# Block 0's down-projection added by ScalarE copies and DMA additions, and the attention's bias made later in seven pieces

## The chip, the cores and the metric

The kernel runs on one core of one Trainium2 chip. The metric is the device time of one execution in microseconds (us), given as a median of several runs. Lower is better. The engines are named as the profile names them: PE is TensorE, DVE is VectorE, ACT is ScalarE, POOL is GpSimd, and SP is the queue that issues most loads.

## The reference

A decoder trunk of two layers on one sequence of 512 tokens with 1024 features, all in float32. Each layer does, in this order:

```python
x = x + 0.5 * swiglu(rms_norm(x, ffn1_norm[l]), ffn1_wg[l], ffn1_wu[l], ffn1_wd[l])
h = rms_norm(x, mix_norm[l]); z = h @ w_in[l]      # [q | k | v | conv_B | conv_C | conv_h]
x = x + concat([attention(q, k, v, sink), short_conv(B, C, h_conv)]) @ w_out[l]
x = x + 0.5 * swiglu(rms_norm(x, ffn2_norm[l]), ffn2_wg[l], ffn2_wu[l], ffn2_wd[l])
```

and a final `rms_norm` ends it. `swiglu(h, wg, wu, wd)` is `(silu(h @ wg) * (h @ wu)) @ wd` with 2816 inner features. The attention has 8 query heads, works in blocks of 128 tokens with a window of 128, and adds to the scores a bias that depends on the head and on the distance of query and key alone; keys outside the window get a very large negative number. That bias, 8 heads x 128 queries x 256 keys, is made once by the kernel.

## The kernel before

The stream x lies in SBUF with features on partitions: eight tiles `xs[c]` of 128 features x 512 tokens. Every product is done with float32 split in two parts (high and low, `hi` and `lo`), three matmuls for one: weights are split by `split` (L224: an ACT cast makes `wh`, a DVE subtraction makes `wl`), activations likewise.

**The stages of a SwiGLU.** `INNER` lists them: `p` (two blocks of 128 inner features done plainly), `d (0,)` (block 0's part of the down-projection, eight column results of 128 features, three matmuls per row chunk), then five stages `w` 1, 3, 5, 7, 9, two `s` stages and a last `d`. A stage `w` is a product of gate and up weights done with seven products in place of eight (`winograd2`, in the order of `CHAINS`: operands b11, b21, t2, t3, t1, t4, b22). Each of its seven products has two halves of 12 matmuls (L806), 168 in all. This text calls the stages w1, w3, w5. The first products of a `w` stage are added up in PSUM under the names `x` (tag `mm`), `w` (tag `aux`) and `y` (tag `sc`); tags `sc` and `aux` have two buffers each.

**Block 0's down-projection in the first SwiGLU.** `down(rhs, fresh=True)` yields eight results `acc`. The first four lie in tag `mm`, the last four in `sc`, `sc`, `aux`, `aux`. For each, DVE does `xs[c] = 0.5 * acc + xs[c]` (L1228), and between them the operands of w1 are made (`norm.make`: half-size sums on DVE at L587 to L592, splits at L224). The normed input is scaled on DVE at L536 just before. The stream is next read or written in the last stages of the same SwiGLU: what the `s` stages yield is kept apart (`Apart`) and added at the end.

**The weights.** Each `w` stage needs ten weight tiles of 512 KB; `need_raw` loads them by SP (L207) some tiles ahead, and sums of two weight blocks are made by a second DMA issued by POOL which adds to the tile in SBUF (L219), or by DVE (L263, L283). There are eight tiles (`raw`), three `wh` and three `wl`. `take_split` hands out the next split and has the splits of two groups ahead traced. `state["rest"]` is the last DVE subtraction of a split that was traced; `tc.issue_after(i)` queues what the block traces for an engine behind instruction `i` on that engine. For all else a scheduler decides at build time, from the order in which instructions are traced and from its own estimates, in what order each engine gets them; each engine then works through its list in order.

**The attention's bias.** `make_bias` (L769 to L782) makes it: an iota on POOL (L771), a conversion on DVE (L773), two masks and their sum (L776 to L778), and eight operations, one for each head (L780). It is traced at once ahead of w3 in the first SwiGLU (`late()`, where `b == 3`). Its first reader is the attention of the first layer, after that SwiGLU.

Temporary tiles come from `g2` (14 buffers of 128 x 512 float32) and `nsq` (2 buffers of that size, used by the squares of the norms).

Of the kernel before, what the change touches and what calls it, by code (L numbers as in the profile page):

```python
# [8 lines left out]
F32 = mybir.dt.float32  # L9
# [3 lines left out]
I32 = mybir.dt.int32  # L13
AF = mybir.ActivationFunctionType
ALU = mybir.AluOpType

P = 128
# [4 lines left out]
NH = 8  # L22
# [5 lines left out]
FAR = -3.0e38  # L28
# [4 lines left out]
INNER = (  # L33
    ("p", 0), ("d", (0,)), ("w", 1), ("w", 3), ("w", 5), ("w", 7), ("w", 9), ("s", 1), ("s", 5),
    ("d", (9, 10)),
)
# [37 lines left out]
def trunk_kernel(  # L74
# [23 lines left out]
    nc = tc.nc  # L98
# [5 lines left out]
    work = ctx.enter_context(tc.tile_pool(name="work", bufs=1))  # L104
# [5 lines left out]
    def g2(name, dt=F32, shape=(P, S)):  # L110
        return work.tile(list(shape), dt, tag="g2", bufs=14, name=name)
# [63 lines left out]
    def turn_rows(i):  # L175
        n = rows[i].shape[0]
        rp = psum("aux", [P, n], f"par_ps{i}")
        nc.tensor.transpose(rp, rows[i], ident[:n, :n])
        nc.scalar.copy(par[:, 16 * i : 16 * i + n], rp)
# [15 lines left out]
    state = {"raw": 0, "split": 0, "group": 0, "late": None}  # L195
# [228 lines left out]
    xs = [xpair[c // 2][:, c % 2, :] for c in range(KC)]  # L424
# [181 lines left out]
    norm = Norm(0)  # L606
# [159 lines left out]
    bias_f = const.tile([P, NH * P], F32, name="bias")  # L766
    bias = bias_f.bitcast(BF16).rearrange("p (h k) -> p h k", h=NH)

    def make_bias():  # L769
        di = g2("dist_i", I32, (P, 2 * P))  # L770
        nc.gpsimd.iota(di, pattern=[[-1, 2 * P]], base=P, channel_multiplier=1)  # L771
        df = g2("dist", F32, (P, 2 * P))
        nc.vector.tensor_copy(df, di)  # L773
        m0 = g2("mask0", F32, (P, 2 * P))
        m1 = g2("mask1", F32, (P, 2 * P))
        nc.vector.tensor_scalar(m0, df, 0.0, FAR, op0=ALU.is_lt, op1=ALU.mult)  # L776
        nc.vector.tensor_scalar(m1, df, float(P), FAR, op0=ALU.is_ge, op1=ALU.mult)
        nc.vector.tensor_add(m0, m0, m1)  # L778
        for h in range(NH):
            nc.vector.scalar_tensor_tensor(  # L780
                bias[:, h, :], df, -(2.0 ** -(h + 1)), m0, op0=ALU.mult, op1=ALU.add
            )  # L782

    def stand(accs, wh, wl, xh, xl, h, start):

# [124 lines left out]
    def ahead(ops, at):  # L910
        return lambda step: ops.make(*at.get(step, ()))


    def ffn(norm, stages, after=None, late=None):
# [207 lines left out]
        def shared(b):  # L1122
            return Seven(lambda: [raws[b], raws[b + 2]], room_form, f"s_{norm.i}_{b}")

        def joined(between):


            def step(n):
                if n == 3:
                    crossing[0].join_half(0)  # L1130
                if n == 4:
                    crossing.pop(0).join_half(1)
                if crossing and isinstance(crossing[-1], Tail):
                    crossing[-1].during(n)
                between(n)

            return step
# [17 lines left out]
        def flush(n=1, *tag):  # L1155
            for _ in range(n):
                if pending:
                    pending.pop(0)(*tag)

        end = None  # L1160
        kept = {}
        apart = Apart(f"{norm.i}")
        for i, (what, b) in enumerate(stages):
            if what == "w" and stages[i + 1][0] == "s":
                ops = shared(sevens[0])
                winograd2(b, ahead(ops, {3: ("b11",), 4: ("b21",), 5: ("t2",), 6: ("t3",)}))
            elif what == "w":
                if late and b == 3:
                    late()
                if after is None and b == 1:  # L1170
                    end = apart = Finale()
                winograd2(b, end and b == 1 and end.step)
            if what == "s" and end:
                ends = [
                    Seven(full, None, f"e_{n}")
                    for n, full in enumerate((lambda b=b: [raws[b + 4], raws[b + 6]], raws[b + 8]))
                ]

                def between(step):
                    if 0 < step < 3:  # L1180
                        flush(2, "mm")
                    for at, n, operand in ((3, 0, "b11"), (4, 1, "b11"), (5, 0, "t2"), (6, 1, "t2")):
                        if step == at:
                            ends[n].make(operand)

                share(ops, 0.5, joined(between), apart, still=kept)
            elif what == "e":
                end.last(ends, kept)
                return
            elif what == "s" and b == sevens[0]:  # L1190
                then = shared(sevens[1])
                share(
                    ops,
                    0.5,
                    joined(ahead(then, {3: ("b11",), 4: ("b21",), 5: ("t2",), 6: ("t3",)})),
                    apart,
                    still=kept,
                )
            elif what == "s":

                def between(step):
                    if step == 1:
                        crossing[0].rejoin(1)
                    if step in (4, 5):
                        with tc.issue_after(state["rest"]):
                            crossing[0].parts(step - 4)
                    if step in SENT_AT:
                        apart.send(*SENT_AT[step])
                    if step == 6:
                        apart.back(1, 1)  # L1210

                share(then, 0.5, between, apart, behind=(0, 2, 3), on=kept)
            if what == "p":
                plain(b)
                if late:
                    turn_rows(1)
            if what != "d":
                continue
            rhs = [(acts[k][0][:, j, :], acts[k][1][:, j, :]) for k in b if k in acts for j in range(2)]
            final = i + 1 == len(stages)  # L1220
            if final:
                after.norm.order = halves_of(KC, 1, True)
            for c, acc in down(rhs, b == (0,), final):
                if b == (0,):
                    made = {0: "b21", 2: "t2", 5: "t3"}
                    if c in made:
                        norm.make(made[c])
                nc.vector.scalar_tensor_tensor(  # L1228
                    xs[c], acc, 0.5, xs[c], op0=ALU.mult, op1=ALU.add
                )  # L1230
                flush()
                if final:
                    for quarter in BACK_AT.get(c, ()):
                        apart.back(*quarter)
                    for k in FINAL_AT.get(c, (c,)):
                        after(k)

    class Finale:
# [7 lines left out]
        def step(self, step):  # L1246


            if step > 2:
                return  # L1250
            for t, tag in (((0, "sc"),), ((1, "sc"),), ((2, "mm"), (3, "aux")))[step]:
                tps = []
                for half in range(2):
                    tp = psum(tag, [P, S], f"yt_{t}_{half}")
                    for j in range(NT):
                        nc.tensor.transpose(
                            tp[:, j * P : (j + 1) * P],
                            xs[half * NT + j][:, t * P : (t + 1) * P],
                            ident,
                        )  # L1260
                    tps.append(tp)
                if t == 0:
                    self.y.append([bias_f[:, half * S : (half + 1) * S] for half in range(2)])
                if t == 1:
                    self.y.append([g2(f"ytok{t}_{half}") for half in range(2)])
                if t > 1:
                    self.late.append(tps)
                else:
                    for half in range(2):
                        nc.scalar.copy(self.y[t][half], tps[half])  # L1270
            if step == 2:
                for t, tps in zip((2, 3), self.late):
                    room = xpool.tile([P, 2, S], F32, tag=f"x{t}", name=f"ytok{t}")
                    self.y.append([room[:, half, :] for half in range(2)])
                    for half in range(2):
                        nc.scalar.copy(self.y[t][half], tps[half])
# [379 lines left out]

    for l in range(DEPTH):
        n1, n2, n3 = Norm(3 * l + 1), Norm(3 * l + 2), Norm(3 * l + 3)
        ffn(norm, INNER, into(n1), None if l else make_bias)
        mix(l, n1, into(n2))  # L1660
        if l + 1 < DEPTH:
            ffn(n2, INNER, into(n3))
        else:
            ffn(n2, LAST)
        norm = n3
# [30 lines left out]
```

## Time and profile before

| | |
|---|---|
| median of 3 runs | 1644.7 us (1643.36 to 1645.09) |
| the profiled execution | 1644.6 us |
| its span, first to last instruction | 1642.8 us |
| granted clock of TensorE | 0.999 |
| DVE busy | 1375.2 us |
| ACT busy | 1169.0 us |
| HBM read | 264.29 MB |

The profile is one execution taken by the hardware profiler. A row of the timeline has start, length, engine, line, operation, output <- inputs, and in brackets how long the engine stood idle before it and who ended that. A row of the waits has who waited on whom, the time in all, how often, and the longest. A row of a line's or a tile's instructions has min/median/max of their length in ns. A row of windows has the stretch, its length, and the busy time of PE, the weight loads, DVE, ACT and POOL in it (instructions in brackets), the clock, the busy share of the DMA engines, and GB/s.

### The profile page before, as it was taken

Reading aid. Unit: us, or ns where it says so; the run is one execution under the profiler, and the core shown is the slowest. Engines: PE = TensorE matmul, PEld = TensorE weight load, DVE = VectorE, ACT = ScalarE, POOL = GpSimd, SP = SyncE. Lnnn points to the kernel's source line nnn. Section 1 sums busy time; section 2 is a strip of 40 time slices with the busy share of each in tenths; the row PEclk is TensorE's granted clock in tenths of the full one; section 3 lists DMA queues with packets and bytes.
Section 4 is the critical chain, followed back from the end, with each engine's and each line's share of the span. In section 5 each row is a group of like instructions: output and inputs, shape, how many; then the busy total and the mean of one; then the engine's idle time right before and its main releaser. Section 6 shows DMA issues by size and latency. Waiting matters only on the chain.

```text
span 1642.8 us, 21157 instructions
## 1 busy us (share of the span) xinstructions
PE 1623.4 (99%) x7588; PEld 1349.7 (82%) x7588; DVE 1375.2 (84%) x1787; ACT 1169.0 (71%) x1498; POOL 216.5 (13%) x191
## 2 busy tenths in 40 slices
PE   9899999999999999999999999999999999999998
PEld 6678888888898888888888888888888988888886
DVE  7977797887899977798999777979788998777997
ACT  6557778766767577777865777788586766777665
POOL 1011111100131011111011111110012111111121
PEclk9999999999999999999999999999999999999999
DMA  9489989932497699999966989998136967999992
GB/s 270 124 209 224 229 212 232 222 100 62 110 222 191 176 227 216 213 214 234 238 150 173 228 208 216 217 230 231 52 90 151 230 146 187 222 222 225 231 266 71
DMA packets 301789, 314.96 MB, mean 192 GB/s; under 512 B 121260, under 2 KB 184308, under 8 KB 301684
## 3 DMA queue, kind: packets, MB, share of 16 engines
q1 hardware_dynamic: 260916, 229.58, 49.6%
q0 software_dynamic: 40048, 83.37, 29.8%
q8 instruction: 59, 0.97, 0.2%
q10 hardware_dynamic: 720, 0.66, 0.1%
q14 instruction: 46, 0.38, 0.1%
HBM read 264.29 MB, written 2.10 MB: 162 GB/s over the span
## 4 chain that ended last, share of the span: by engine, by line
PE 80%; DVE 9%; ACT 5%; DMA 3%; issue 2%; POOL 0%; SPq 0%; ACTq 0%; DVEq 0%; POOLq 0%
PE x L806 25%; PE y L806 13%; PE x_s L806 7%; PE w L806 6%; PE acc L311 4%; PE acc L310 4%; PE acc L313 4%; PE y_s L806 4%; DVE wl L224 3%; PE w_s L806 2%; PE x_m L791 2%; ACT wh L224 1%; PE y_m L791 1%; PE acc L684 1%; PE x_e L806 1%
## 5 line engine op out<-in xcount | busy, mean ns | idle before, releaser
L224 DVE TENSOR_TENSOR wl<-raw,wh 128x1024 fp32r<-128x1024 f32 (+1 forms) x493 | 599.3, 1223 | 176.1 <-ACT wh L224 175.0
L224 ACT CAST wh<-raw 128x1024 fp32r<-128x1024 f32 (+1 forms) x493 | 513.2, 1045 | 307.3 <-PE x L806 100.4
L311 PE MATMUL acc<-xl,wh 128*128 128x512 f32 x392 | 153.4, 391 | 0.3 <-DVE xl L457 0.3
L310 PE MATMUL acc<-xh,wh 128*128 128x512 f32 x392 | 153.1, 392 | 0.5 <-ACT wh L224 0.5
L313 PE MATMUL acc<-xh,wl 128*128 128x512 f32 x384 | 149.8, 390 | 0.0
L219 POOL DMA_DIRECT2D raw<-in_ffn_wu_dram x40 | 50.5, 1270 | 402.7 <-DMA raw<-in_ffn_wu_dram 273.0
L311 PEld LDWEIGHTS acc<-xl,wh 128*128 128x128 f32 x392 | 73.7, 188 | 15.5 <-DVE xl L457 1.0
L310 PEld LDWEIGHTS acc<-xh,wh 128*128 128x128 f32 x392 | 73.8, 188 | 15.2 <-ACT wh L224 0.6
L313 PEld LDWEIGHTS acc<-xh,wl 128*128 128x128 f32 x384 | 72.2, 188 | 14.9
L219 POOL DMA_DIRECT2D raw<-in_ffn_wg_dram x40 | 49.4, 1265 | 201.6 <-DMA raw<-in_ffn_wu_dram 74.9
L219 POOL DMA_DIRECT2D raw<-in_ffn_wd_dram x34 | 41.2, 1220 | 246.3 <-DVE wl L224 103.0
L263 DVE TENSOR_TENSOR raw<-raw,raw 128x1024 f32<-128x1024 f32 x58 | 70.4, 1219 | 3.1 <-DMA raw<-in_ffn_wu_dram 2.6
L806 PE MATMUL w<-wh,fb21h 128*128 128x512 f32 x160 | 62.5, 391 | 2.1 <-DVE x L1228 2.1
L806 PE MATMUL w<-wl,fb21h 128*128 128x512 f32 x160 | 62.3, 391 | 1.5 <-DVE wl L224 1.5
L1068 ACT COPY raw_a<-turned 128x1024 uint16<-128x1024 uint16 x48 | 63.5, 1356 | 0.0
L806 PE MATMUL y<-wh,ft3h 128*128 128x512 f32 x160 | 62.4, 390 | 0.9 <-ACT wh L224 0.9
L806 PE MATMUL x<-wl,ft2h 128*128 128x512 f32 x160 | 62.2, 390 | 1.1 <-DVE wl L224 1.1
L806 PE MATMUL x<-wl,fb11h 128*128 128x512 f32 x160 | 62.2, 390 | 1.0 <-DVE wl L224 1.0
L806 PE MATMUL y<-wh,ft4h 128*128 128x512 f32 x160 | 62.3, 390 | 0.5 <-ACT wh L224 0.5
L806 PE MATMUL x<-wh,ft2h 128*128 128x512 f32 x160 | 62.4, 390 | 0.0
L806 PE MATMUL x<-wh,ft2l 128*128 128x512 f32 x160 | 62.3, 389 | 0.0
L806 PE MATMUL w<-wh,fb21l 128*128 128x512 f32 x160 | 62.3, 389 | 0.0
(501 smaller groups left out, 4532.3 us busy)
## 6 DMA issues: line engine op xcount, KB each, us to landing
raw<-in_ffn_wu_dram SPq DMA_DIRECT2D x127, 512.0 KB, 5.3
raw<-in_ffn_wd_dram SPq DMA_DIRECT2D x105, 512.0 KB, 6.2
raw<-in_ffn_wg_dram SPq DMA_DIRECT2D x86, 512.0 KB, 5.3
raw<-in_ffn_wu_dram POOLq DMA_DIRECT2D x40, 512.0 KB, 8.6
raw<-in_ffn_wg_dram POOLq DMA_DIRECT2D x40, 512.0 KB, 6.1
raw<-in_w_in_dram SPq DMA_DIRECT2D x36, 512.0 KB, 3.8
raw<-in_ffn_wd_dram POOLq DMA_DIRECT2D x34, 512.0 KB, 9.6
raw<-raw POOLq DMA_DIRECT2D x21, 512.0 KB, 7.0
```

What stands on the lines that cost most here:

```text
L219: nc.gpsimd.dma_start(out=r, in_=rows_of(*more), accum_op=ALU.add)
L224: return nc.scalar.copy(hi, raw), eng.tensor_sub(lo, raw, f32(hi))
L263: nc.vector.tensor_add(a11, a11, s1)
L310: nc.tensor.matmul(acc, hi[:, k, :], rhs[k][0], start=k == first, stop=False)
L311: nc.tensor.matmul(acc, hi[:, k, :], rhs[k][1], start=False, stop=False)
L313: nc.tensor.matmul(acc, lo[:, k, :], rhs[k][0], start=False, stop=k == last)
L684: nc.tensor.matmul(opening[n], (lo if part == "w" else hi)[:, k, :], xl if part == "x" else xh, start=n not in begun, stop=k == KC - 1 and ...
L791: nc.tensor.matmul(accs[c // 2][:, c % 2, :], w[:, k, cols], x_[:, 2 * h + k, :], start=start and c % 2 == 0 and h + k + i == 0, stop=h + ...
L806: nc.tensor.matmul(accs[u], x_[:, 2 * h + k, tok], w[:, k, :], start=start and h + k + i == 0, stop=h + k == 2 and i == 2, skip_group_chec ...
L1068: nc.scalar.copy(words(raws[self.b][:, c, :]), self.to[:, :, c, :])
```

## The change

Two things are changed, both in the first SwiGLU of the first layer only.

1. For block 0's down-projection, ACT copies 0.5 * `acc` from PSUM into a new `g2` tile, and a DMA issued by POOL adds that tile to `xs[c]` in SBUF. The DVE instruction stays for all other places.
2. `make_bias` becomes `bias_steps`, which returns a function that `winograd2` calls after each of the seven steps of w5 (`b == 5`). After step 0 it traces the iota, the conversion and the masks; after steps 1 to 6 the heads (0, 1), (2, 3), 4, 5, 6, 7. Each piece's DVE instructions are queued behind the last DVE split traced. `dist` and `mask0` move from `g2` to `nsq`.

```diff
-    def make_bias():
+    def bias_steps():
...
-                if late and b == 3:
-                    late()
                 if after is None and b == 1:
                     end = apart = Finale()
-                winograd2(b, end and b == 1 and end.step)
+                between = late if b == 5 else end.step if end and b == 1 else None
+                winograd2(b, between)
...
-                nc.vector.scalar_tensor_tensor(
-                    xs[c], acc, 0.5, xs[c], op0=ALU.mult, op1=ALU.add
-                )
+                if b == (0,) and norm.i == 0:
+                    part = g2(f"down_{c}")
+                    nc.scalar.activation(part, acc, AF.Copy, scale=0.5)
+                    nc.gpsimd.dma_start(out=xs[c], in_=part, accum_op=ALU.add)
+                else:
+                    nc.vector.scalar_tensor_tensor(
+                        xs[c], acc, 0.5, xs[c], op0=ALU.mult, op1=ALU.add
+                    )
```

The new function, where `masks` holds what `make_bias` did up to the sum of the masks and `heads` the operation of L780:

```python
        def step(n):
            with tc.issue_after(state["rest"]):
                if n == 0:
                    masks()
                else:
                    heads(*((0, 1), (2, 3), (4,), (5,), (6,), (7,))[n - 1])
```

More of the change, by code (lines that the diff above doesn't have):

```diff
@@ L767, in trunk_kernel, with masks, heads, step @@
     bias = bias_f.bitcast(BF16).rearrange("p (h k) -> p h k", h=NH)
-    def make_bias():
[L770 to L781, printed above, removed]
-            )
+    def bias_steps():
+        made = {}
+        def masks():
+            di = g2("dist_i", I32, (P, 2 * P))
+            nc.gpsimd.iota(di, pattern=[[-1, 2 * P]], base=P, channel_multiplier=1)
+            df = work.tile([P, 2 * P], F32, tag="nsq", bufs=2, name="dist")
+            nc.vector.tensor_copy(df, di)
+            m0 = work.tile([P, 2 * P], F32, tag="nsq", bufs=2, name="mask0")
+            m1 = g2("mask1", F32, (P, 2 * P))
+            nc.vector.tensor_scalar(m0, df, 0.0, FAR, op0=ALU.is_lt, op1=ALU.mult)
+            nc.vector.tensor_scalar(m1, df, float(P), FAR, op0=ALU.is_ge, op1=ALU.mult)
+            nc.vector.tensor_add(m0, m0, m1)
+            made["m"] = df, m0
+        def heads(*hs):
+            df, m0 = made["m"]
+            for h in hs:
+                nc.vector.scalar_tensor_tensor(
+                    bias[:, h, :], df, -(2.0 ** -(h + 1)), m0, op0=ALU.mult, op1=ALU.add
+                )
+        def step(n):
+            with tc.issue_after(state["rest"]):
+                if n == 0:
+                    masks()
+                else:
+                    heads(*((0, 1), (2, 3), (4,), (5,), (6,), (7,))[n - 1])
+        return step
     def stand(accs, wh, wl, xh, xl, h, start):
@@ L1227, in ffn @@
                         norm.make(made[c])
-                nc.vector.scalar_tensor_tensor(
-                    xs[c], acc, 0.5, xs[c], op0=ALU.mult, op1=ALU.add
-                )
+                if b == (0,) and norm.i == 0:
+                    part = g2(f"down_{c}")
+                    nc.scalar.activation(part, acc, AF.Copy, scale=0.5)
+                    nc.gpsimd.dma_start(out=xs[c], in_=part, accum_op=ALU.add)
+                else:
+                    nc.vector.scalar_tensor_tensor(
+                        xs[c], acc, 0.5, xs[c], op0=ALU.mult, op1=ALU.add
+                    )
                 flush()
@@ L1658, in trunk_kernel @@
         n1, n2, n3 = Norm(3 * l + 1), Norm(3 * l + 2), Norm(3 * l + 3)
-        ffn(norm, INNER, into(n1), None if l else make_bias)
+        ffn(norm, INNER, into(n1), None if l else bias_steps())
         mix(l, n1, into(n2))
```

## The prediction

> **What bounds the kernel now.** First the page's head, for the size of the field; then busy time by stage of block 0 and the blocks behind it.
>
> ```profile
> span 1642.8 us, 21157 instructions
> PE 1623.4 (99%) x7588; PEld 1349.7 (82%) x7588; DVE 1375.2 (84%) x1787; ACT 1169.0 (71%) x1498; POOL 216.5 (13%) x191
> ```
> ```profile
> 45.40:90.00 44.60, 39.66 (x170) 30.98 (x169) 41.89 (x44) 24.20 (x29) 2.39 (x2) 1.00 0.51 138
> 90.00:130.90 40.90, 38.73 (x170) 31.38 (x169) 31.14 (x41) 27.22 (x32) 5.64 (x6) 1.00 0.87 218
> 130.90:169.00 38.10, 38.10 (x170) 31.56 (x169) 27.71 (x29) 28.12 (x33) 4.90 (x5) 1.00 0.93 221
> ```
>
> TensorE (PE) is busy 99% of the span, so only its gaps can be won: 1642.8 - 1623.4 = 19.4 us in all. The windows are the first three seven-product stages of the first SwiGLU, w1, w3 and w5 (columns after the stretch: its length, busy us of PE, weight loads, VectorE = DVE, ScalarE = ACT, POOL, then clock, DMA share, GB/s). All three do the same 168 matmuls. w5 has no gap; w1 and w3 have 4.9 and 2.2 us. In w1 DVE works 41.89 of 44.60 us, in w5 27.71 of 38.10. A gap costs more than it shows, since the matmuls behind it start slowly; so I take the stages' lengths from PE's timeline, whose first matmul of each of four stages is:
>
> ```profile
> 45.37 0.39 PE L806 MATMUL x<-wh,fb11h 128*128 128x512 f32 x1
> ...
> 89.98 0.39 PE L806 MATMUL x<-wh,fb11h 128*128 128x512 f32 x1
> ...
> 130.88 0.39 PE L806 MATMUL x<-wh,fb11h 128*128 128x512 f32 x1
> ...
> 168.96 0.39 PE L806 MATMUL x<-wh,fb11h 128*128 128x512 f32 x1
> ```
>
> w1 lasts 44.61, w3 40.90, w5 38.08 us. Against w5, w1 loses **6.53** and w3 **2.82**, together 9.35 us: the most that the change can win here. The waits of PE in these stages name who ends them:
>
> ```profile
> PE x L806 <- DVE wl L224: 2.1, 2, 1.1
> PE w L806 <- DVE x L1228: 2.1, 1, 2.1
> PE w L806 <- DVE wl L224: 1.5, 2, 1.1
> PE y L806 <- ACT wh L224: 1.4, 2, 0.9
> ```
>
> The 2.1 on L1228 is the PSUM room of the `w` chain: the last two column results of block 0 sit in it until DVE has added them to the stream. DVE's timeline shows why that is late:
>
> ```profile
> 43.12 1.27 DVE L1228 SCALAR_TENSOR_TENSOR x<-acc,x 128x512 f32<-128x512 f32 x2
> ...
> 46.60 0.68 DVE L1228 SCALAR_TENSOR_TENSOR x<-acc,x 128x512 f32<-128x512 f32 x1
> ...
> 48.93 1.21 DVE L224 TENSOR_TENSOR wl<-raw,wh 128x1024 fp32r<-128x1024 f32 x1
> ...
> 53.00 1.88 DVE L1228 SCALAR_TENSOR_TENSOR x<-acc,x 128x512 f32<-128x512 f32 x3
> ...
> 77.94 1.22 DVE L224 TENSOR_TENSOR wl<-raw,wh 128x1024 fp32r<-128x1024 f32 x1 [1.43 <-ACT wh L224]
> ```
> ```profile
> L1228 DVE SCALAR_TENSOR_TENSOR x<-acc,x 128x512 f32<-128x512 f32 x8 | 5.2, 679 | 0.0
> ```
>
> The second block is the group of these instructions between 40 and 90 us (busy, mean ns, idle before). DVE has not one idle gap in the timeline's stretch before the 1.43 us at 77.94. So w1 is bound by DVE's queue: whatever leaves it brings forward everything behind it.
>
> **The additions.** Removed: the eight L1228 instructions. One lasts 0.68 us, three in a row 1.88 (at 53.00), so they start 0.60 us apart, and 8 x 0.60 = 4.8 us leave DVE. Added: eight ACT copies out of PSUM, and eight DMA additions issued by POOL.
>
> ```profile
> L870 ACT ACTIVATE apart<-x_s x18: 583/596/604, 249.4 to 1091.2; 128x512 f32<-128x512 f32 x18
> ```
> ```profile
> 40.41 1.04 ACT L224 CAST wh<-raw 128x1024 fp32r<-128x1024 f32 x1
> 43.23 1.06 ACT L224 CAST fb21h<-hf 128x1024 fp32r<-128x1024 f32 x1 [1.78 <-DVE hf L536]
> 45.38 1.06 ACT L224 CAST wh<-raw 128x1024 fp32r<-128x1024 f32 x1 [1.10 <-PE acc L311]
> 48.10 1.05 ACT L224 CAST wh<-raw 128x1024 fp32r<-128x1024 f32 x1 [1.66 <-PE x L806]
> ...
> 58.31 1.05 ACT L224 CAST ft1h<-hf 128x1024 fp32r<-128x1024 f32 x1 [5.36 <-DVE hf L590]
> ```
>
> L870 is the same operation on the same shape: 0.596 us, 8 x 0.596 = 4.8 us. ACT is idle 1.78 + 1.10 + 1.66 = 4.5 us between 41.45 and 48.10 and 5.36 us ahead of 58.31, so the copies lie beside other work. They empty PSUM as the columns end (the last just before w1's first matmul at 45.37), so the `w` chain finds its room free. Without that cover a copy ahead of a cast costs 0.6 us.
>
> Is all of the 4.8 us won? The two additions at 43.12 stood where DVE had to wait anyway: the next step needs the cast `fb21h` of 43.23, which ends at 44.29. Their 1.2 us are won only if other ready work moves in. There is some: the `wl` of 48.93 needs the `wh` cast at 40.41, long done, and takes 1.14 us. I take it that it moves in, and subtract 0.1 for an ACT copy ahead of the cast at 45.38: **4.7 us**. The ends: 2.4 (gap not filled, two copies ahead of `fb21h`: 4.8 - 1.2 - 1.2) and 6.53 (the last stalls vanish as well, because DVE falls behind PE less).
>
> POOL and the DMA queues. The rows are POOL's timeline, the nearest DMA addition between SBUF tiles, the software queue of the page, and three 10 us windows:
>
> ```profile
> 39.18 2.47 POOL L219 DMA_DIRECT2D raw<-in_ffn_wg_dram  x2 [2.26 <-DMA raw<-in_ffn_wu_dram]
> 79.52 1.19 POOL L219 DMA_DIRECT2D raw<-in_ffn_wu_dram  x1 [37.88 <-DVE wl L224]
> ```
> ```profile
> L230 POOL DMA_DIRECT2D wl<-raw x10: 856/896/899, 36.0 to 1334.4; - x10
> ```
> ```profile
> q0 software_dynamic: 40048, 83.37, 29.8%
> ```
> ```profile
> 40.00:50.00 10.00, 9.15 (x41) 7.25 (x39) 10.00 (x13) 5.46 (x6) 1.57 (x2) 1.00 0.74 125
> 50.00:60.00 10.00, 7.31 (x29) 5.30 (x30) 10.00 (x12) 3.76 (x6) 0.00 (x0) 1.00 0.01 2
> 60.00:70.00 10.00, 9.11 (x40) 7.09 (x40) 10.00 (x11) 7.97 (x11) 0.00 (x0) 1.00 0.13 32
> ```
>
> Eight issues of at most 0.90 us (the row is 512 KB, these are 256) fill 7.2 of the 37.88 us in which POOL waits; no weight addition is due behind them before 79.52. The data: 29.8% of 1642.8 is 490 us for 83.37 MB, 5.9 us a MB; 8 x 256 KB are 2.1 MB, an estimate of **12.3 us** of all DMA engines. From 40 to 70 they stand idle 2.6 + 9.9 + 8.7 = 21.2 us, because the weight buffers are full; with DVE 4.8 us earlier some 16 us are left. The additions land by about 57, loads resume about 64, and the code reads the stream next in the last stage of this SwiGLU, far behind. Cost 0; the eight `g2` buffers are held until landing, while w1 needs its own ones later. What an addition of this size takes is bounded by 0 and by the 12.3 us in the way of the loads (a rival below).
>
> **The bias leaves w3.** Its rows on DVE and POOL:
>
> ```profile
> 95.67 0.29 DVE L773 CAST dist<-dist_i 128x256 f32<-128x256 int32 x1 [1.65 <-POOL dist_i L771]
> 95.88 1.22 DVE L224 TENSOR_TENSOR wl<-raw,wh 128x1024 fp32r<-128x1024 f32 x1
> ...
> 100.03 2.77 DVE L780 SCALAR_TENSOR_TENSOR bias<-dist,mask 128x256 bf16<-128x256 f32 x8
> 102.71 2.35 DVE L224 TENSOR_TENSOR wl<-raw,wh 128x1024 fp32r<-128x1024 f32 x2
> ```
> ```profile
> 92.85 2.42 POOL L219 DMA_DIRECT2D raw<-in_ffn_wg_dram  x2 [10.79 <-DMA raw<-in_ffn_wu_dram]
> 94.77 0.87 POOL L771 IOTA dist_i<- 128x256 int32 x1
> ...
> 130.46 2.46 POOL L219 DMA_DIRECT2D raw<-in_ffn_wg_dram  x2 [9.22 <-DVE raw L263]
> 155.92 1.20 POOL L219 DMA_DIRECT2D raw<-in_ffn_wu_dram  x1 [22.99 <-DMA raw<-in_ffn_wu_dram]
> ```
>
> DVE stood 1.65 us before the cast of `dist`, because the iota was queued on POOL behind two weight additions. The `wl` of 95.88 could have started at 94.0 (95.67 - 1.65) and ended at 95.2. PE asks for it about 95.9 (89.98 and 26 matmuls of 38.08 / 168 = 0.227 us), so 0.6 us are to spare. The second stall is the `wl` of 102.71 behind 2.77 us of heads. Both go: **2.8 us**. If the weight DMAs that end about 92 (POOL's row waits 10.79 us for one) come over 0.6 us later against PE, the first half stays: lower end 1.4.
>
> **The bias comes to w5**, on DVE behind the last split traced: masks (four operations of about the 0.29 us of the cast's row, 1.0 us as I take it), then 2.77 us of heads in six pieces of 0.7 or 0.35 us. DVE idles 38.10 - 27.71 = 10.4 us in w5, so 3.8 us fit; the waits that end those gaps are for ACT casts which wait for PE's buffers, so a piece delays a `wl` by under 1 us where w5 showed no stall. The iota, if it follows the pair of 130.46, ends about 133.8; the masks follow the first step, after 136.3 (130.88 and 24 matmuls). Cost 0, at most 1.1 (one stall of w3's size).
>
> **Sum.** The profiled execution took 1644.6 us, 1.8 around its span; the median of the runs is 1644.7. 1644.6 - 4.7 - 2.8 + 0 = **1637.1 us**. PE's waits list none from w5's start to 290 us, so I count nothing later.
>
> **Rivals.**
> - *The order on DVE doesn't close up* (17%): the gap at 43.1 stays, copies delay `fb21h`. w1 gains 2.4 to 3.6: 1638.2 to 1639.4. For it: the order is fixed before the run by a scheduler that I don't see.
> - *Everything goes* (13%): 1644.6 - 9.35 = 1635.2 to about 1636.2. Against it: two of PE's waits end by ACT casts, and those rows of ACT above wait for PE themselves.
> - *ScalarE becomes the bound* (11%): ACT works in order, and a copy that waits for a late column holds back the casts behind it; w1 keeps its 6.5 us and only the bias pays: 1641.8, give or take 1.5. Against it: the idle time in ACT's rows above.
> - *The additions land late and collide* (7%): they start only when DVE first idles, and their 12.3 us fall on the weight loads of w3. Its weight addition then lands up to 12.3 us late, less 0.6 spare, so PE loses 11.7: 1637.1 + 11.7 = 1648.8, slower than before. It decides from about 8 us of overlap. Against it: at 39.18 the two issues took 2.47 us together while DVE was 10.00 of 10.00 busy. The Trainium skill says why such a delay could be ("SBUF — State Buffer", section "SBUF: two separate sides"): DVE in a two-port mode locks GpSimd out of the port through which it writes DMA descriptors. By that rule the additions would wait out DVE's work in w1; the row at 39.18 speaks against it for the operations that run here, hence only 7%.
> - *The iota is queued behind the next block's additions* (4%), those of 155.92 and the one after it, and so ends about 159 (155.92 + 2 x 1.20 + 0.87). DVE stands at the cast of `dist`; PE runs out of `wl` at the third product (130.88 + 48 x 0.227 = 141.8) and loses some 18 us: 1655. Against it: those additions are traced some three steps later.
>
> **Chances.** The forecast, 1636.2 to 1638.1, has 48%. A measurement of this kernel can tell about 0.2%, 3.3 us, from no change: faster is below 1641.4. Faster 80% (48 + 17 + 13 and a little of the third rival), within 9%, slower 11%. The range from 1635.2 to 1641.0 leaves out most of the ScalarE case and the two slow ones.
>
> **What would show it.** Right: w1 about 39.9 us long and no wait of PE on L1228 or its successor; w3 and w5 both about 38.1; POOL with eight additions between 41 and 52 whose landing ends before 60. Wrong: waits of PE for `wh` in w1 behind the new copies; DVE idle before 45; w3's first half-sum waiting longer for its DMA; DVE waiting for `dist_i` in w5; new waits behind 170 us, where I expect none.

## The result, and the profile after

The changed kernel takes **1636.93 us** (median of 7 runs, 1634.12 to 1641.58), the kernel before 1644.7 us (7 runs, 1643.19 to 1647.15). The ratio is **0.9956**, 95% interval 0.994 to 0.9972: faster by 0.44%. The profiled execution took 1636.5 us, 8.1 less than the one of before.

The head of the page of the changed kernel, then its windows over w1, w3 and w5, and the first matmul of each of four stages on PE's timeline. Lines of the matmuls are 16 higher than before (L822 was L806).

```profile
span 1634.7 us, 21179 instructions
PE 1621.7 (99%) x7588; PEld 1350.2 (83%) x7588; DVE 1369.8 (84%) x1779; ACT 1172.0 (72%) x1506; POOL 223.5 (14%) x199
```
```profile
45.00:84.80 39.80, 38.66 (x169) 31.18 (x168) 37.35 (x37) 24.82 (x31) 6.36 (x7) 1.00 0.84 205
84.80:122.90 38.10, 38.10 (x169) 31.53 (x168) 27.67 (x29) 26.97 (x32) 4.81 (x4) 1.00 0.95 233
122.90:161.00 38.10, 38.10 (x170) 31.55 (x169) 30.69 (x40) 28.12 (x34) 5.22 (x5) 1.00 0.98 220
```
```profile
44.95 0.39 PE L822 MATMUL x<-wh,fb11h 128*128 128x512 f32 x1
...
84.82 0.39 PE L822 MATMUL x<-wh,fb11h 128*128 128x512 f32 x1
...
122.90 0.39 PE L822 MATMUL x<-wh,fb11h 128*128 128x512 f32 x1
...
160.98 0.39 PE L822 MATMUL x<-wh,fb11h 128*128 128x512 f32 x1
```

| stage | before | after | won |
|---|---|---|---|
| up to w1's first matmul | 45.37 | 44.95 | 0.42 |
| w1 | 44.61 | 39.87 | 4.74 |
| w3 | 40.90 | 38.08 | 2.82 |
| w5 | 38.08 | 38.08 | 0 |

Together they are 7.98 us. The 0.42 is no work of the change: in the execution before, PE waited 1.0 us for a load of x, and this one did not. Of PE's waits of before between 40 and 130 us none is left. There is one new one, at the third product of w1:

```profile
PE x L822 <- DVE wl L224: 1.1, 1, 1.1
```

The 7.98 do not simply stay until the end. The lead over the kernel before is 9.50 us when the next such stage begins (at 528.95 us), 9.82 at 852.11, 8.30 at 1335.46, and 8.1 at the end. Between the last two PE has two waits in the second layer that the execution of before has not, 1.43 us together; the first is

```profile
1147.93 0.50 PE L311 MATMUL acc<-xl,wh 128*128 128x512 f32 x1 [1.13 <-DVE xl L457]
```

Two further profiled executions of the changed kernel do not have them, and their lead at the same place is 10.68 and 10.37 us. The gain behind w5 is in all three; whether the change makes it is not shown, since only one execution of the kernel before was profiled.

On DVE's timeline of w1 the eight additions are gone, and the `wl` that stood at 48.93 has moved into the first of the gaps they left:

```profile
41.75 1.41 DVE L536 SCALAR_TENSOR_TENSOR hf<-x,par,inv 128x512 f32<-128x512 f32 x2
43.08 1.22 DVE L224 TENSOR_TENSOR wl<-raw,wh 128x1024 fp32r<-128x1024 f32 x1
44.21 1.22 DVE L587 TENSOR_TENSOR sums<-hf,hf 128x1024 f32<-128x1024 f32 x1
...
72.99 1.22 DVE L224 TENSOR_TENSOR wl<-raw,wh 128x1024 fp32r<-128x1024 f32 x1 [1.35 <-ACT wh L224]
```

The row at 72.99 stood at 77.94 before: DVE's queue lies 4.95 us earlier, of which 0.42 are the earlier start of w1. ACT's timeline has the copies in its former idle time, POOL's the eight additions, and two rows of their line say how long one takes from issue to landing:

```profile
39.03 0.60 ACT L1245 ACTIVATE down<-acc 128x512 f32<-128x512 f32 x1 [2.64 <-PE acc L332]
...
40.47 1.58 ACT L1245 ACTIVATE down<-acc 128x512 f32<-128x512 f32 x3
...
44.27 1.62 ACT L1245 ACTIVATE down<-acc 128x512 f32<-128x512 f32 x3
45.71 1.11 ACT L224 CAST wh<-raw 128x1024 fp32r<-128x1024 f32 x1
```
```profile
41.42 6.67 POOL L1246 DMA_DIRECT2D x<-down  x7
48.28 0.86 POOL L1246 DMA_DIRECT2D x<-down  x1 [0.19 <-issue]
74.52 1.21 POOL L219 DMA_DIRECT2D raw<-in_ffn_wu_dram  x1 [25.39 <-DVE wl L224]
```
```profile
L1246 POOL DMA_DIRECT2D x<-down x8: 856/2013/2549, 41.4 to 48.3; - x8
...
DMA to landing us min/median/max: 7.6/9.9/11.0
```

The cast behind the last three copies starts at 45.71 (45.38 before). The last addition, issued at 48.28, lands about 58 at the median of 9.9 us. The software queue between 40 and 62 us (packets, MB, share of 16 engines):

```profile
q0 software_dynamic: 1738, 3.25, 82.8%
```

In w5 the iota follows the pair of weight additions on POOL at once, and DVE's pieces lie between splits:

```profile
125.32 0.94 POOL L774 IOTA dist_i<- 128x256 int32 x1
```
```profile
131.52 0.29 DVE L776 CAST dist<-dist_i 128x256 f32<-128x256 int32 x1
...
135.05 0.75 DVE L787 SCALAR_TENSOR_TENSOR bias<-dist,mask 128x256 bf16<-128x256 f32 x2
135.72 1.22 DVE L224 TENSOR_TENSOR wl<-raw,wh 128x1024 fp32r<-128x1024 f32 x1
138.40 1.23 DVE L224 TENSOR_TENSOR wl<-raw,wh 128x1024 fp32r<-128x1024 f32 x1 [1.47 <-ACT wh L224]
```

The cast of `dist` starts with no wait for POOL, and behind the pieces DVE has its gaps of 1.5 us again.

### The profile page after: what moved, and what is told of

It is laid out like the page before. It is cut to its first block, busy times and chain, and to the rows that moved or that the text cites. A ratio compares the mean times of both kernels' runs of the same rounds, so it can differ in the third digit from the quotient of the medians.

```text
span 1634.7 us, 21179 instructions
## 1 busy us (share of the span) xinstructions
PE 1621.7 (99%) x7588; PEld 1350.2 (83%) x7588; DVE 1369.8 (84%) x1779; ACT 1172.0 (72%) x1506; POOL 223.5 (14%) x199
## 4 chain that ended last, share of the span: by engine, by line
PE 89%; DVE 5%; ACT 3%; issue 1%; DMA 1%; ACTq 0%; DVEq 0%
PE x L822 26%; PE y L822 13%; PE x_s L822 8%; PE w L822 6%; PE acc L310 6%; PE acc L311 6%; PE acc L313 5%; PE y_s L822 5%; PE x_m L807 3%; PE w_s L822 3%; DVE wl L224 1%; PE y_m L807 1%; PE y_e L822 1%; PE acc L684 1%; PE x_e L822 1%
## 5 line engine op out<-in xcount | busy, mean ns | idle before, releaser
L263 DVE TENSOR_TENSOR raw<-raw,raw 128x1024 f32<-128x1024 f32 x58 | 70.5, 1220 | 5.0 <-DMA raw<-in_ffn_wu_dram 3.5
L822 PE MATMUL x<-wl,ft2h 128*128 128x512 f32 x160 | 62.2, 390 | 1.1 <-DVE wl L224 1.1
L822 PE MATMUL y<-wh,ft4h 128*128 128x512 f32 x160 | 62.4, 390 | 0.1
L822 PE MATMUL x<-wh,ft2h 128*128 128x512 f32 x160 | 62.3, 390 | 0.0
L822 PE MATMUL w<-wh,fb21h 128*128 128x512 f32 x160 | 62.3, 390 | 0.0
L822 PE MATMUL y<-wh,ft3h 128*128 128x512 f32 x160 | 62.3, 390 | 0.0
L822 PE MATMUL x<-wh,ft1h 128*128 128x512 f32 x160 | 62.3, 389 | 0.0
L822 PE MATMUL x<-wh,ft2l 128*128 128x512 f32 x160 | 62.3, 389 | 0.0
L822 PE MATMUL x<-wh,ft1l 128*128 128x512 f32 x160 | 62.3, 389 | 0.0
L822 PE MATMUL w<-wl,fb21h 128*128 128x512 f32 x160 | 62.3, 389 | 0.0
```

The costliest lines, as they stand in the source:

```text
L263: nc.vector.tensor_add(a11, a11, s1)
L822: nc.tensor.matmul(accs[u], x_[:, 2 * h + k, tok], w[:, k, :], start=start and h + k + i == 0, stop=h + k == 2 and i == 2, skip_group_chec ...
```

## The experiments

The lengths of w1, w3 and w5 are from the first matmuls of the stages in each kernel's profiled execution. They agree within 0.1 us between executions of one kernel, where whole times differ by 2 us and more, so they carry the argument. The kernel before was run again beside each of the three groups of experiments; its medians there were 1646.0, 1645.09 and 1643.88 us, so a time of one run says little by itself.

| kernel | w1 | w3 | w5 |
|---|---|---|---|
| before | 44.61 | 40.90 | 38.08 |
| changed kernel | 39.87 | 38.08 | 38.08 |
| additions alone | 39.85 | 40.72 | 38.08 |
| bias alone | 44.58 | 38.08 | 38.08 |
| copies, added by DVE | 45.08 | 38.08 | 38.08 |
| copies, added by POOL itself | 51.70 | 38.08 | 38.08 |
| pieces in w3 | 39.86 | 38.08 | 38.08 |
| bias at once ahead of w5 | 39.85 | 38.08 | 38.37 |
| every addition twice | 42.38 | 38.08 | 38.08 |
| bias at once ahead of w3, early iota | 39.90 | 39.68 | 38.08 |
| w1's operands later | 38.19 | 38.08 | 38.08 |

**The additions alone**

```diff
-                between = late if b == 5 else end.step if end and b == 1 else None
+                if late and b == 3:
+                    late(None)
+                between = end.step if end and b == 1 else None
```

`late(None)` makes the masks and all heads at once, with its tiles in `g2`, as `make_bias` did.

> Only the additions are changed; the bias is made at once ahead of w3, as before. Theory (w1 is bound by DVE's queue, the two parts add up): w1 39.9 us as in the changed kernel, w3 40.9 as before, w5 38.1; some 4.7 us under before, about 1639.9 where before is 1644.6. Rival (the shorter w1 is worth something only together with the bias moved, since the loads of w3 then come late against PE): w3 over 42 us.

Measured: 1640.42 us, ratio 0.9965 (0.9953 to 0.9977). w1 is as short as with both parts, and w3 loses what it lost before. The rival falls.

**The bias alone**, the DVE instruction kept everywhere:

```diff
-                if b == (0,) and norm.i == 0:
-                    part = g2(f"down_{c}")
-                    nc.scalar.activation(part, acc, AF.Copy, scale=0.5)
-                    nc.gpsimd.dma_start(out=xs[c], in_=part, accum_op=ALU.add)
-                else:
+                if True:
                     nc.vector.scalar_tensor_tensor(
```

> Only the bias is moved to w5 in seven pieces; DVE adds block 0's results as before. Theory: w1 44.6, w3 38.1, w5 38.1 us, about 2.8 us under before. Rival (w3's first stall is the late weight addition and not the iota): w3 39.3 to 39.5 and a wait of PE for wl of about 1 us left.

Measured: 1641.11 us, ratio 0.9979 (0.9967 to 0.9991); w3 has no stall left, w1 has its old one. So the parts add up, stage by stage: 4.76 and 2.82 us. The wait for PSUM room is back in PE's waits of this kernel:

```profile
PE w L822 <- DVE x L1244: 2.1, 1, 2.1
```

**PSUM room or DVE's queue?**

```diff
-                    nc.gpsimd.dma_start(out=xs[c], in_=part, accum_op=ALU.add)
+                    nc.vector.tensor_add(xs[c], xs[c], part)
```

> ACT copies block 0's results out of PSUM as in the changed kernel, but DVE adds the copies to the stream (eight 128x512 additions from SBUF) in place of the DMAs. So PSUM comes free as early, and DVE has as much to do as before. Theory (DVE's queue is the bound): w1 43 to 44.6 us, 3 to 4.8 us over the changed kernel. Rival (what counted was the PSUM room that the w chain waited 2.1 us for): w1 at most 42.3, with most of the gain kept.

Measured: 1645.77 us in its one run. The `w` chain no longer waits for room: its first matmul starts 5.4 us earlier than in the kernel before. And yet w1 is 45.08 us, longer than before. First that matmul and the `wl` of the chain in the kernel before, then the matmul here, DVE's timeline and PE's first wait of that chain:

```profile
54.43 0.47 PE L806 MATMUL w<-wh,fb21h 128*128 128x512 f32 x1 [2.10 <-DVE x L1228]
54.80 2.35 DVE L224 TENSOR_TENSOR wl<-raw,wh 128x1024 fp32r<-128x1024 f32 x2
```
```profile
49.04 0.39 PE L822 MATMUL w<-wh,fb21h 128*128 128x512 f32 x1
```
```profile
43.53 1.28 DVE L1246 TENSOR_TENSOR x<-x,down 128x512 f32<-128x512 f32 x2
...
53.36 1.88 DVE L1246 TENSOR_TENSOR x<-x,down 128x512 f32<-128x512 f32 x3
55.16 2.35 DVE L224 TENSOR_TENSOR wl<-raw,wh 128x1024 fp32r<-128x1024 f32 x2
```
```profile
56.43 0.50 PE L822 MATMUL w<-wl,fb21h 128*128 128x512 f32 x1 [3.67 <-DVE wl L224]
```

The eight additions stand nearly where they stood, the `wl` behind them comes at 55.16 (54.80 before), and PE waits for that in place of the room. The 2.1 us wait named in the profile of before was only the name of what came last; the bound was DVE's queue. This is the clearest verdict of the study. It does not say that the additions had to leave DVE: no run lets DVE add the copies later, in a stage where it has room (in w5 it idles 10.4 us).

**The additions by POOL's own arithmetic**

```diff
-                    nc.gpsimd.dma_start(out=xs[c], in_=part, accum_op=ALU.add)
+                    nc.gpsimd.tensor_add(xs[c], xs[c], part)
```

> The eight copies are added to the stream by POOL itself (tensor_add, some 2.0 us each by the row of the last norm) and not by DMA. Theory: POOL waits for nothing else here, 16 us of it end before its next weight addition at 74.5, so w1 is 39.9 us as in the changed kernel. Rival (POOL and DVE shut each other out of a common port while both read two SBUF tiles): DVE's 1.22 us operations or its gaps grow, up to 16 us in all, and w1 is 42 us or more.

Measured: 1649.46 us in its one run, w1 51.70. POOL's and DVE's timelines, and PE's:

```profile
41.59 6.67 POOL L1246 TENSOR_TENSOR x<-x,down 128x512 f32<-128x512 f32 x5
```
```profile
41.12 8.23 DVE L224 TENSOR_TENSOR fb11l<-hf,fb11h 128x1024 fp32r<-128x1024 f32 x1 [0.25 <-ACT fb11h L224]
```
```profile
49.41 0.79 PE L822 MATMUL x<-wh,fb11l 128*128 128x512 f32 x1 [3.55 <-DVE fb11l L224]
```

One subtraction that takes 1.22 us elsewhere took 8.23: it ended at 49.35, about its own length after POOL's five additions in a row (48.26). The rival holds, by its mechanism; part of the 51.70 us is also the lower clock that followed PE's wait (last section). The issue of DMA additions beside the same DVE work had no such cost (eight in 7.7 us, and every subtraction of DVE in w1 at its usual 1.22), so of these two ways of using POOL only the DMA works.

**Is it the cutting up, or the place?** Pieces in w3:

```diff
-                between = late if b == 5 else end.step if end and b == 1 else None
+                between = late if b == 3 else end.step if end and b == 1 else None
```

> The changed kernel with the seven pieces of the bias made in w3 in place of w5. Theory (cutting it up is what counts: a piece of 0.35 to 1.2 us fits in DVE's gaps, and the masks come behind a split that is traced two groups ahead): w3 38.1 to 38.3 us, w5 38.1, no wait of PE for wl in w3. Rival (the place counts: w3's half-sum waits 1.4 us for its weight addition, which leaves DVE too little room): w3 39 us or more.

Measured: w3 38.08 us, as the theory has it; 1634.28 us in its one run. The pieces are not only cut, they also come later: the cast of `dist` starts 10.3 us after the stage's start and waits for nothing, where with the additions alone it starts after 5.5 us and waits for the iota. The run does not tell the two apart. The opposite, made at once ahead of w5, with `late(None)` as in the first experiment:

```diff
-                between = late if b == 5 else end.step if end and b == 1 else None
+                if late and b == 5:
+                    late(None)
+                between = end.step if end and b == 1 else None
```

> The changed kernel with the bias made at once ahead of w5, as it was made ahead of w3 before, not in pieces. Theory (cutting it up is what counts): w5 40 to 41 us with one or two waits of PE for wl of about 1 us, w1 39.9 and w3 38.1. Rival (the place counts): w5 38.1.

Measured: w5 38.37 us, 1635.0 us in its one run. That misses the theory: made at once in w5, the same work costs 0.3 us and not 2 to 3. So cutting up is not what counts by itself; each of the two remedies would do nearly alone. Why w3 is different is seen when the same rows of DVE and POOL of two kernels are set beside each other. First the additions alone, bias ahead of w3 (which starts at 87.58), then this kernel, bias ahead of w5 (which starts at 122.92):

```profile
89.59 1.23 DVE L263 TENSOR_TENSOR raw<-raw,raw 128x1024 f32<-128x1024 f32 x1 [0.84 <-DMA raw<-in_ffn_wu_dram]
...
93.11 0.29 DVE L776 CAST dist<-dist_i 128x256 f32<-128x256 int32 x1 [1.69 <-POOL dist_i L774]
93.32 1.22 DVE L224 TENSOR_TENSOR wl<-raw,wh 128x1024 fp32r<-128x1024 f32 x1
```
```profile
90.25 2.45 POOL L219 DMA_DIRECT2D raw<-in_ffn_wg_dram  x2 [10.68 <-DMA raw<-in_ffn_wu_dram]
92.24 0.84 POOL L774 IOTA dist_i<- 128x256 int32 x1
```
```profile
123.62 1.22 DVE L263 TENSOR_TENSOR raw<-raw,raw 128x1024 f32<-128x1024 f32 x1
...
126.10 0.29 DVE L776 CAST dist<-dist_i 128x256 f32<-128x256 int32 x1 [0.65 <-POOL dist_i L774]
126.31 1.22 DVE L224 TENSOR_TENSOR wl<-raw,wh 128x1024 fp32r<-128x1024 f32 x1
```
```profile
123.22 2.48 POOL L219 DMA_DIRECT2D raw<-in_ffn_wg_dram  x2 [10.39 <-DVE wl L224]
125.23 0.83 POOL L774 IOTA dist_i<- 128x256 int32 x1
```

The order is the same. In w3 the `wl` starts 5.74 us after the stage's start, in w5 3.39. The 2.35 us between them have two parts. The half-sum (L263) starts 1.31 us later after the stage's start, and in w3 it waits for a weight DMA. The cast waits 1.04 us longer for the iota, which POOL has queued behind two weight additions; in w3 these wait for a DMA. So weight DMAs come late in w3. The reason is argued, not shown: the loads stand still for most of w1 and seem to be behind when w3 begins, but no run moves them.

**The share of the iota**

```diff
+        di = work.tile([P, 2 * P], I32, tag="nsq", bufs=2, name="dist_i")
+        nc.gpsimd.iota(di, pattern=[[-1, 2 * P]], base=P, channel_multiplier=1)
         def masks():
-            di = g2("dist_i", I32, (P, 2 * P))
-            nc.gpsimd.iota(di, pattern=[[-1, 2 * P]], base=P, channel_multiplier=1)
```

on the kernel with the additions alone, so that the iota is traced ahead of everything.

> The additions as in the changed kernel, the bias at once ahead of w3 as before, but the iota traced at the start, so that DVE never waits for POOL. Theory (the stalls of w3 are the wait for the iota, 1.7 us, and the heads in a row, on top of weight additions that come late): the first wait of PE for wl goes, the second shrinks; w3 38.3 to 39.6 us. Rival (the 3.8 us of DVE work alone are too much for w3): w3 40.5 or more, as with the late iota.

Measured: w3 39.68 us, 1635.8 us in its one run. The wait for POOL and the first stall are gone; the second, behind the heads, is left. Against 40.72 with the late iota, the iota's wait was worth 1.04 us. The other 1.60 (39.68 - 38.08) are the DVE work on top of late weights. Here are the heads in this kernel, where w3 starts at 84.82, and in the one with the bias at once ahead of w5:

```profile
93.66 2.77 DVE L787 SCALAR_TENSOR_TENSOR bias<-dist,mask 128x256 bf16<-128x256 f32 x8
```
```profile
130.45 2.77 DVE L787 SCALAR_TENSOR_TENSOR bias<-dist,mask 128x256 bf16<-128x256 f32 x8
```

They start 8.84 and 7.53 us after their stage's start. The difference, 1.31 us, is also the difference of the two stages' losses (1.60 and 0.29). The measured 39.68 is 0.08 beyond the theory's upper end and 0.82 under the rival's.

**Are the additions really free?** Every addition twice, with 0.25 `acc` (the sum is the same):

```diff
+            twice = []
...
-                    nc.scalar.activation(part, acc, AF.Copy, scale=0.5)
+                    nc.scalar.activation(part, acc, AF.Copy, scale=0.25)
                     nc.gpsimd.dma_start(out=xs[c], in_=part, accum_op=ALU.add)
+                    twice.append((c, part))
+                    if c == KC - 1:
+                        for m, again in twice:
+                            nc.gpsimd.dma_start(out=xs[m], in_=again, accum_op=ALU.add)
```

> The changed kernel with every addition made twice (copies of 0.25 acc, sixteen DMA additions in place of eight), so twice the DMA and POOL work of the additions. The second halves wait for the first to land, so they reach to about 65 us, where the loads of w3 have resumed. Theory (the additions lie in time in which the DMA queues are empty; only what reaches over it can cost): w1 39.9 us, and w3 38.1 to 40, by an overlap of 2 to 5 us less the room there. Rival (the additions cost something already as they are, through POOL or the ports): w1 41 us or more.

Measured: w1 42.38, w3 38.08 us; 1637.61 us in its one run. By its number the rival seems to win, but the rows show the theory's mechanism in another place. ACT's timeline of this kernel, its window from 60 to 70 us, and the same window of the changed kernel:

```profile
71.11 1.04 ACT L224 CAST wh<-raw 128x1024 fp32r<-128x1024 f32 x1 [2.63 <-DMA raw<-in_ffn_wu_dram]
```
```profile
60.00:70.00 10.00, 9.67 (x43) 7.67 (x41) 10.00 (x11) 7.06 (x9) 1.03 (x2) 1.00 1.10 235
```
```profile
60.00:70.00 10.00, 9.94 (x44) 7.86 (x43) 10.00 (x10) 8.53 (x11) 0.00 (x0) 1.00 0.60 190
```

PE's new wait of 2.5 us is for a `wh` whose cast waits for a weight load. With the second eight the DMA engines are full from 60 to 70 us (share 1.10, 0.60 in the changed kernel), and the loads that resume there land late: between 55 and 75 us those of `in_ffn_wu` take 8.0 us from issue to landing at the median, 4.5 in the changed kernel. The one that PE waits for is a load of w1 itself (`wh` of its sixth product), not of w3; so the theory was wrong about w1. One set of additions fits into the pause of the loads; a second reaches over it.

**What is left of w1**

```diff
-                if step < 3:
-                    norm.make(CHAINS[step + 4][1])
+                shift = 1 if norm.i == 0 and b == 1 else 0
+                if shift <= step < 3 + shift:
+                    norm.make(CHAINS[step + 4 - shift][1])
```

> The changed kernel, and w1 makes its operands t1, t4 and b22 one product later than now (after the products 1, 2, 3 in place of 0, 1, 2; they are used in products 4, 5, 6). Theory (what is left of w1's loss, 1.8 us, is again DVE's order: the wl of the third product queues behind the work for t1): the wait of 1.1 us goes, w1 38.1 to 38.5, some 1.5 us under the changed kernel. Rival (DVE has no room at all in w1, and the work only stalls PE later): w1 39.5 to 40.5, with a wait of PE for t1, t4 or b22.

> The changed kernel unchanged, run beside the others for their comparison: 7 to 8 us under before, w1 39.9, w3 and w5 38.1 us.

Measured: w1 38.19 us and no wait of PE left in it, as the theory has it. DVE does as much in w1 as in the changed kernel (37.19 and 37.35 us busy), so what counts is which work stands ahead of a `wl` in its queue, and not only how much DVE has to do. And with the eight DMA additions in it w1 is now within 0.11 us of w5: one set of additions costs no more than that. The whole: 1635.55 us (1633.07 to 1642.98), ratio to before 0.9951 (0.9932 to 0.9969), beside the changed kernel's 1635.06, ratio 0.994 (0.9927 to 0.9953). So both were run once more:

> The kernel of the later operands once more, beside the changed kernel on the same chip, since their medians differed by less than their spread. If the 1.7 us that w1 gained reach the end, its median is 1 to 2 us under the changed kernel; if the scheduler's new order gives them back in the blocks behind, the two agree within 0.5 us, and the starts of the later stages show where.

> The changed kernel unchanged, for the comparison with the later operands: 1635 to 1637 us, w1 39.9, w3 and w5 38.1 us.

Measured: 1634.23 us, ratio 0.9934 (0.9912 to 0.9956), against 1636.13, ratio 0.9948 (0.9927 to 0.9968). w1 is 38.20 again, and in this pair the last SwiGLU stage still starts 1.1 us earlier than in the changed kernel (1566.1 and 1567.2); in the pair ahead it was 0.1 (1566.8 and 1566.9). That w1 gets 1.7 us shorter is shown twice. That the whole gets faster by it is not: one median lies under, one over, and the intervals overlap. Of the 1.36 us of lead that the first pair has behind w5, 0.77 are lost between 1080 and 1333 us, a stretch whose length differs by 2.2 us between executions of the changed kernel. So the question stays open.

## Why the prediction was right

- **The sum.** 1637.1 us forecast, 1636.93 measured; 4.7 and 2.8 us forecast for w1 and w3, 4.74 and 2.82 measured, nothing in w5. Term by term the sum holds up to there. That the whole comes within 0.2 us is partly luck. The prediction counts nothing behind w5, and there the profiled execution gains 1.8 us more and loses 1.7 again. When the same kernel was run twice more, its medians, 1635.06 and 1636.13 us, lay under the forecast's lower end of 1636.2, and it was 10.0 and 7.8 us under the kernel before. Nor are the gaps of 19.4 us the limit that the prediction calls them: w1 had 4.9 us of gaps and lost 6.53, since the slow matmuls behind a gap (0.50 us in place of 0.39) count as busy.
- **The bound of w1.** "Bound by DVE's queue" is shown by the copies that DVE adds: PSUM free early, DVE's load kept, gain gone. The operands made later add that it is the order in this queue that binds. Taking the 4.8 us of the removed instructions, and not the 2.1 us wait that the profile names, was the step that decided.
- **The choice in it.** The `wl` did move into the gap at 43.1, so the first rival (order not closed up) did not come. The cast at 45.38 moved by 0.33 us, and by 0.75 counted from w1's first matmul, not by 0.1; that cost nothing visible.
- **ScalarE.** The copies lie in its idle time; no wait of PE names ACT in w1 any more. That rival falls. One of the signs of being wrong came in small: DVE idles 0.29 us before 40.61, since the cast of `fb11h` stands behind the first copy.
- **The additions' DMA.** 82.8% of 22 us for 3.25 MB are 5.6 us a MB; the estimate was 5.9. Free they are (w1 of 38.19 with the operands later), but the cover is thinner than "some 16 us" against 12.3 sounded: another set costs w1 2.5 us. The collision of the fourth rival is real, though the additions did not start late as it has them. Its place was wrong: it hits w1's own last weights before those of w3.
- **The bias.** Both stalls went, and the sum was right, but the reason was incomplete. I put them down to the iota and to the heads in a row. The same work in the same order costs 0.3 us in w5, so the third part of the cause is that weights come late in w3. The prediction had this only as the risk in its lower end, 1.4. By w5's measure some 0.3 us would have been to win if they had not. The rival with the iota behind the next block's additions did not come: it follows the pair at once.
- **The rule of the Trainium skill** that I weighed ("SBUF — State Buffer", section "SBUF: two separate sides") says that DVE and GpSimd lock each other out of a shared port, and says when: if DVE runs in a two-port mode, or has two SBUF inputs while GpSimd's operation reads SBUF. For DMA issues beside this DVE work the trace showed no lock, and so it came. For POOL's own additions, which read SBUF, beside DVE's with two SBUF inputs the rows look like such a lock, 8.23 us for 1.22. The section gives the port to whichever starts first; here DVE's row starts 0.47 us ahead of POOL's, and yet it ended only after five of POOL's additions.

## What to carry to other kernels

Where an engine has no gap, an instruction that stands ahead of what the next engine waits for costs its own issue distance (here 0.60 us), whatever wait the profile names downstream; the name tells what came last, not what would come last if it were gone. Putting other work later helps in the same way: w1's operands made one product later won 1.68 us of w1. Work moved to another engine is free only in a pause of that engine and of the DMAs it starts, so look up how long the pause is and double the work once to see the edge. And a stall in one stage may have its cause in the stage ahead, as w3's late weights suggest: before cutting work into pieces, ask what makes this place tighter than the next one.

## What the runs showed that I had not expected

**PE ran slower after its two longest waits.** In the two kernels with waits of 3.55 and 3.67 us the granted clock fell behind them. The window of the kernel with POOL's additions from 50 to 60 us, and PE's timeline in the kernel where DVE adds the copies, after its 3.67 us gap:

```profile
50.00:60.00 10.00, 8.46 (x26) 6.42 (x25) 10.00 (x8) 7.01 (x10) 6.22 (x3) 0.73 0.01 2
```
```profile
58.01 0.63 PE L822 MATMUL w<-wh,fb21l 128*128 128x512 f32 x1
58.44 0.63 PE L822 MATMUL w<-wl,fb21h 128*128 128x512 f32 x1
```

The clock is 0.73 in that window, and matmuls start 0.43 us apart in place of 0.227, for 5.7 us in the one kernel and 3.3 us in the other; with gaps of 2.1 us (before) and 2.5 us (additions twice) the clock stayed at 1.00. The Trainium skill ("TensorE: Matmul & The Clock Gate", section "Part 1: The HAM clock gate") has PE's clock halved after an idle window of about 3.4 us, and these four gaps agree. A long gap is not the only case, though: with the additions alone the clock was 0.50 from 10 to 12 us, soon after the start, where no wait of PE was over 1.2 us; what lowered it there is not shown. How much of w1's 45.08 us with the copies added by DVE (44.61 before) is the clock is not shown either: DVE's queue alone lies 0.36 us later in that kernel.

**The start of the kernel varies more than a small change is worth.** w1's first matmul came between 44.92 and 47.73 us in the profiled executions. In the latest, that of the additions alone, PE waited 1.2 us for a load of x and then had the low clock just named. A change of 1 us needs stage lengths, not whole times.
